# Side work of the heads beside a GEMM: asked for at every GEMM step, or at every fifth step only

## The chip, the cores and the metric

The kernel runs on one core of a Trainium2 chip. The metric is the device time of one execution in microseconds, median over several. The engines are TensorE (PE, with PEld for its weight loads), VectorE (DVE), ScalarE (ACT), GpSimd (POOL) and SyncE (SP, which issues the DMAs).

## The reference

One inference step of a two-layer encoder of width 1024 over 640 rows: 512 of one long sequence and 8 short sequences of 16 rows. Each layer:

```python
h = rmsnorm(x); proj = h @ w_in            # u, va, q|k|v, z, beta, decay, two gates
z_a = gelu(u) * gmlp_spatial(layernorm(gelu(va)))
q, k, v = silu(causal_conv(qkv))           # 8 heads of 128, q and k normalised
o, S = gated_delta_rule(q, k, v, g, beta, s0)
z_b = rmsnorm(o) * silu(z)
x += (sigmoid(ga) * (z_a @ p_a) + sigmoid(gb) * (z_b @ p_b)) @ w_o
x += relu(rmsnorm(x) @ w_up)**2 @ w_down
```

The gated delta rule works per head in four chunks of 128 rows (the kernel's t = 0 to 3) and one tile of the eight short sequences (t = 4). Inside a chunk a unit lower triangular system is solved, then a state S of 128x128 goes from chunk to chunk:

```python
vnew = U - W @ S                 # kS, y, w in the kernel
o    = qg @ S + P @ vnew         # o
S    = S * decay + kg.T @ vnew   # S
```

## The kernel before

GEMMs are made at higher precision: a weight block `raw` (128x1024, one DMA of 512 KB) is split by ScalarE into `whi` (L131) and by VectorE into the rest `wlo` (L132). The activations are split likewise into Ah and Al. `three` then issues for each of 8 k-slices and 2 halves of the columns three matmuls of 128x320: whi by Ah, whi by Al, wlo by Ah. One such triple is a *GEMM step*; a block has 16 steps and a pair of PSUM banks (tag g, two pairs). `Feed` keeps up to two raw tiles loaded ahead and one block split ahead.

The stage `heads` of a layer takes 10 *slots*, h = 0 to 9. A slot has the GEMM blocks of head h (names pg_p, the q, k and v columns, followed by their convolution: cb, then yb at L461, three VectorE passes of 128x664) and some gate blocks (names pg_g, followed by sg at L812). A slot has n = 16 steps for each of its blocks: 64, 112, seven times 80, and 96. Beside the GEMM of slot h run, as Python generators:

- `gating` in slot 0 (decays and betas of all heads),
- `prepare` of head h-1: transposes (ps_kt, kg), the products (ps_gp, AP), a row-wise solve on VectorE (dg, Bs, pr, X), at its end n0c and m16, then the small products Y3 (m16 by q32, copied by ScalarE to y32 at L597) and Z3 (n0c by y32, added to n0c by VectorE at L600). In the profile names these tiles are ps_Y, ps_Z and y. Before the end of prepare the Exp of the next head's decays (E) are issued on ScalarE,
- `chain` of head h-2: the rest of the inverse (Y, M1, Z, Y2, N2), then the recurrence over t: kS, y, w (copied by ScalarE at L662), S with o (the new S is written by VectorE, L734 for t = 0, L732 after). `sample()` runs beside it: kS4, qS4, w4, o4, the scaled copies `we` (ScalarE L699, POOL L700), and S4 in two halves, each added to the state by VectorE (L705),
- `roots` of head h-3: the norm's squares so (L752, L753), their split sh, and means.

Each generator yields a number: how many of its own units the part is that it has just issued. `paced` spreads `length` units (CHAIN 66, PREPARE 70, GATING 48, for roots n; in slot 9 chain and roots in turn, 92) over the n steps of the slot. Before each GEMM step the loop at L913 asks chain, roots and prepare in this order, and each issues what is due. What is left at the slot's end is issued by `run` after the last step. TensorE's instructions stand in the program's order. The other engines' order is set by a scheduler that goes by priority, and `paced` gives side work a lead by `tc.high_priority` (400 for the chain, 200 for prepare and gating, 1 for roots). PSUM banks for the side work: tag c (chain) and tag d (all others), two each.

Of the kernel before, what the change touches and what calls it, by code (L numbers as in the profile page):

```python
# [62 lines left out]
def encoder(ctx, tc, xin, wblk, wba, sct, sdelta, prow, pcol, gates, wst, bsr, convw, consts, delta0,  # L63
# [161 lines left out]
    def paced(work, n, ahead=AHEAD):  # L225


        length, gen = work
        due = 0
        for u in range(n):  # L230
            while due * n <= u * length:
                with tc.high_priority(offset=ahead):
                    due += next(gen, length)
            yield
        run(gen)
# [6 lines left out]
    def run(*gens):  # L242

        for _ in gens[0]:
            for g in gens[1:]:
                next(g, None)
# [562 lines left out]
    def heads(l, ond, msd, gd, close, norm):  # L809
# [70 lines left out]
        with phase(f"heads{l}", 1) as pl:  # L880
# [15 lines left out]
            for h, slot in enumerate(heads_blocks()):  # L896

                n = 16 * len(slot)
                work = []
                if h == H + 1:  # L900
                    work.append(paced((CHAIN + ROOTS, in_turn(
                        chain(l, h - 2, pl, out["gate"], out), lambda: roots(l, h - 2, pl, ond, msd, out))), n, 2 * AHEAD))
                elif h >= 2:
                    work.append(paced((CHAIN, chain(l, h - 2, pl, out["gate"], out)), n, 2 * AHEAD))
                if h >= 3:
                    work.append(paced((n, roots(l, h - 3, pl, ond, msd, out)), n, 1))
                if 1 <= h <= H:
                    work.append(paced((PREPARE, prepare(l, h - 1, pl, act, out["gate"], out)), n))
                if h == 0:
                    work.append(paced((GATING, gating(l, pl, pl, out)), n))  # L910
                for b in slot:
                    stream = gemm(l, b, *how[b])
                    for _ in range(16):  # L913
                        for w in work:
                            next(w)
                        next(stream)
                    run(stream)
                for w in work:
                    run(w)
# [295 lines left out]
```

## Time and profile before

| | us |
|---|---|
| median of three runs | 2545.5 (2544.97 to 2547.24) |
| the profiled execution | 2544.76 |
| its span, first to last instruction | 2543.0 |
| head stage of layer 0, from 54.5 to 569.4 | 514.9 |
| head stage of layer 1, from 1309.0 to 1821.6 | 512.6 |
| TensorE busy over the span | 2471.5 |

All rows of the prediction are from this one execution. A row of the timeline has the start in us, the duration, engine, line, operation, out<-in, the tile's shape and a count; in brackets stands the idle time before it on its engine and what released it. A pair of matmuls of the side work is one row (x2), a group of 16 small ones is one row too (x32, since each counts twice). Matmuls overlap, so the distance of two starts, not the duration, is what one costs. The table of waits has the instruction that waits, what it waits for, the time in all, how often, and the longest.

### The profile page before, as it was taken

What the parts mean: (1) busy time and instruction counts of PE and PEld (TensorE: products, weight loads), DVE (VectorE), ACT (ScalarE), POOL (GpSimd) and SP (SyncE); (2) the same over time, 40 slices, a digit from 0 to 9 for tenths busy, and PEclk for the clock granted to TensorE, in tenths of its full rate; (3) what the DMA queues carried; (4) which work ended last, traced back from release to release, by engine and by line L of the source; (5) the groups of instructions that cost most, each with busy time, mean ns of one, the idle gap of its engine ahead of it and who ended that gap; (6) DMA issues with size and microseconds to landing.
All of it is one profiled execution on the core that took longest, in us unless ns stands there. A gap on an engine that the chain in (4) does not pass through costs nothing. (4 is left out here: it accounts for less than half of the span.)

```text
span 2543.0 us, 45063 instructions
## 1 busy us (share of the span) xinstructions
PE 2471.5 (97%) x18456; PEld 2392.6 (94%) x18456; DVE 1306.3 (51%) x2677; ACT 1011.2 (40%) x1952; POOL 652.6 (26%) x673
## 2 busy tenths in 40 slices
PE   7999999999999999999999999999989999999997
PEld 7899999997899999999999999999979999999997
DVE  7656677535556433333356677674274553333333
ACT  4656666533223212121346666664332222122122
POOL 3223443213422201010213343331253221011012
PEclk9999999999999999999999999999999999999998
DMA  4223433336432222222233333333554322222221
GB/s 161 90 95 101 127 94 95 115 121 229 149 116 75 67 76 76 75 76 75 81 102 108 101 99 95 95 117 117 159 201 142 96 68 76 75 76 76 77 72 66
DMA packets 124238, 261.29 MB, mean 103 GB/s; under 512 B 17232, under 2 KB 56048, under 8 KB 124032
## 3 DMA queue, kind: packets, MB, share of 16 engines
q1 hardware_dynamic: 124032, 258.41, 31.9%
q8 instruction: 145, 2.38, 0.4%
q14 instruction: 61, 0.50, 0.1%
HBM read 218.22 MB, written 40.15 MB: 102 GB/s over the span
## 5 line engine op out<-in xcount | busy, mean ns | idle before, releaser
L131 ACT ACTIVATE whi<-raw 128x1024 fp32r<-128x1024 f32 x304 | 322.1, 1060 | 1012.0 <-issue 367.7
L132 DVE TENSOR_TENSOR wlo<-raw,whi 128x1024 fp32r<-128x1024 f32 x304 | 405.1, 1332 | 161.0 <-ACT whi L131 146.6
L80 PE MATMUL pg_dn<-gl,whi 128*128 128x320 f32 x1024 | 316.6, 309 | 2.1 <-DVE gl L1085 2.1
L80 PE MATMUL pg_up<-Ah,whi 128*128 128x320 f32 x1024 | 317.1, 310 | 0.0
L80 PE MATMUL pg_dn<-gh,whi 128*128 128x320 f32 x1024 | 316.7, 309 | 0.0
L80 PE MATMUL pg_up<-Ah,wlo 128*128 128x320 f32 x1024 | 316.4, 309 | 0.0
L80 PE MATMUL pg_dn<-gh,wlo 128*128 128x320 f32 x1024 | 316.4, 309 | 0.0
L80 PE MATMUL pg_up<-Al,whi 128*128 128x320 f32 x1024 | 316.4, 309 | 0.0
L80 PE MATMUL pg_g<-Ah,whi 128*128 128x320 f32 x896 | 290.8, 325 | 0.0
L80 PE MATMUL pg_g<-Ah,wlo 128*128 128x320 f32 x896 | 278.3, 311 | 7.5 <-DVE wlo L132 7.5
L80 PE MATMUL pg_g<-Al,whi 128*128 128x320 f32 x896 | 277.7, 310 | 0.0
L1084 POOL TENSOR_TENSOR r<-r 128x640 f32<-128x640 f32 x64 | 101.8, 1590 | 684.8 <-ACT gh L1083 684.8
L80 PE MATMUL pg_p<-Ah,whi 128*128 128x320 f32 x768 | 252.1, 328 | 0.0
L80 PE MATMUL pg_p<-Ah,wlo 128*128 128x320 f32 x768 | 237.3, 309 | 0.0
L80 PE MATMUL pg_p<-Al,whi 128*128 128x320 f32 x768 | 236.8, 308 | 0.0
L80 PEld LDWEIGHTS pg_dn<-gl,whi 128*128 128x128 f32 x1024 | 192.2, 188 | 2.6 <-DVE gl L1085 2.6
L80 PEld LDWEIGHTS pg_up<-Al,whi 128*128 128x128 f32 x1024 | 192.2, 188 | 0.0
L80 PEld LDWEIGHTS pg_up<-Ah,whi 128*128 128x128 f32 x1024 | 192.2, 188 | 0.0
L80 PEld LDWEIGHTS pg_dn<-gh,whi 128*128 128x128 f32 x1024 | 192.2, 188 | 0.0
L80 PEld LDWEIGHTS pg_dn<-gh,wlo 128*128 128x128 f32 x1024 | 192.2, 188 | 0.0
L80 PEld LDWEIGHTS pg_up<-Ah,wlo 128*128 128x128 f32 x1024 | 192.2, 188 | 0.0
L80 PEld LDWEIGHTS pg_g<-Ah,wlo 128*128 128x128 f32 x896 | 169.5, 189 | 8.1 <-DVE wlo L132 8.1
(703 smaller groups left out, 5473.5 us busy)
## 6 DMA issues: line engine op xcount, KB each, us to landing
raw<-in_wblk SPq DMA_DIRECT2D x304, 512.0 KB, 3.6
gd<-sg SPq DMA_DIRECT2D x56, 320.0 KB, 2.4
rg<-gd SPq DMA_DIRECT2D x48, 320.0 KB, 2.9
S<-in_sdelta SPq DMA_DIRECT2D x16, 512.0 KB, 6.5
out<-S SPq DMA_DIRECT2D x16, 512.0 KB, 3.5
gr<-rowd SPq DMA_DIRECT2D x16, 320.0 KB, 4.9
er<-rowd SPq DMA_DIRECT2D x16, 320.0 KB, 3.2
ond<-osb SPq DMA_DIRECT2D x16, 320.0 KB, 2.2
```

Of the source, the lines that this page charges most:

```text
L80: nc.tensor.matmul(out, lhsT=lhsT, rhs=rhs, start=start, stop=stop, **kw)
L131: nc.scalar.activation(dst_hi, src, AF.Copy)
L132: nc.vector.tensor_tensor(dst_lo, src, dst_hi.bitcast(F32), op=ALU.subtract)
L1084: nc.gpsimd.tensor_tensor(r[:], r[:], r[:], op=ALU.mult)
```

## The change

`paced` looks whether parts are due at steps 0, 5, 10 and so on only. Parts that fell due at the steps between are issued together at the next such step, for chain, roots, prepare and gating alike, and what fell due after the last such step is issued at the end of the slot.

```diff
@@ paced(work, n, ahead)
         length, gen = work
         due = 0
         for u in range(n):
-            while due * n <= u * length:
+            while u % 5 == 0 and due * n <= u * length:
                 with tc.high_priority(offset=ahead):
                     due += next(gen, length)
             yield
```

In a slot of 80 steps the parts stand at these steps (80 is the slot's end):

| part | before | after |
|---|---|---|
| means (ps_ms), first and second | 8, 18 | 10, 20 |
| first w of the chain | 31 | 35 |
| S and o of t = 0 | 36 | 40 |
| kS of t = 1 | 40 | 40 |
| w, S with o of t = 1 | 45, 50 | 45, 50 |
| w4; o4 | 55; 60 | 55; 60 |
| w of t = 3 with the first half of S4 | 74 | 75 |
| Y3 | 76 | 80 |
| S, o of t = 3, second half of S4 | 79 | 80 |
| Z3 | 80 | 80 |

TensorE at the end of slot 7 of layer 0 (names end in head and chunk; 053 is layer 0, head 5, t = 3, ps_S0541 the second half of S4, kt07 the transposes of the next slot). Before:

```order
L80 MATMUL ps_Y306_5648<-m1606_5613,q32_0_87 32x32 x16
L80 MATMUL pg_g204_5563<-Ah_97,whi_5447 128x320
...
L80 MATMUL pg_g204_5563<-Ah_97,wlo_5448 128x320
L80 MATMUL ps_S053_5676<-w05_5629,kg05_4324 128x128
L80 MATMUL ps_o053_5678<-AP05_4408,w05_5629 128x128
L80 MATMUL ps_o053_5678<-qg05_4530,S052_5572 128x128
L80 MATMUL ps_S0541_5685<-we051_5636,k4p05_5502 128x512 x3
L80 MATMUL pg_g204_5563<-Ah_97,whi_5447 128x320
L80 MATMUL pg_g204_5563<-Al_98,whi_5447 128x320
L80 MATMUL pg_g204_5563<-Ah_97,wlo_5448 128x320
L80 MATMUL ps_Z306_5697<-n0c06_5610,y3206_5665 32x32 x16
L498 MATMUL ps_kt07a_5737<-cst_67,kT07_5149 128x128 x4
```

and after, with the last GEMM matmul of the slot first:

```order
L80 MATMUL pg_g204_5557<-Ah_97,wlo_5445 128x320
L80 MATMUL ps_S053_5663<-w05_5632,kg05_4324 128x128
L80 MATMUL ps_o053_5665<-AP05_4432,w05_5632 128x128
L80 MATMUL ps_o053_5665<-qg05_4539,S052_5566 128x128
L80 MATMUL ps_S0541_5672<-we051_5639,k4p05_5496 128x512 x3
L80 MATMUL ps_Y306_5678<-m1606_5613,q32_0_87 32x32 x16
L80 MATMUL ps_Z306_5697<-n0c06_5610,y3206_5695 32x32 x16
L498 MATMUL ps_kt07a_5737<-cst_67,kT07_5149 128x128 x4
```

All GEMM matmuls of the slot now stand ahead of this group, and nothing stands between Y3 and Z3.

ScalarE at the same place, from the last copy w on. Before:

```order
L662 ACTIVATE w05_5629<-ps_w053_5627 128x128
L131 ACTIVATE sh050_5730<-so05_5727 128x320
L699 ACTIVATE we051_5636<-w4p05_5501,mis_78 128x128 x4
L597 ACTIVATE y3206_5665<-ps_Y306_5648 128x128
L666 ACTIVATE osb05_5282<-ps_o053_5678 128x128
L752 ACTIVATE so05_5727<-osb05_5282 128x320
L131 ACTIVATE k4p06_6166<-kg06_5030 128x128
L131 ACTIVATE whi_5754<-raw_0_70_5451 128x1024
L812 ACTIVATE sg204_5694<-pg_g204_5563 128x640
```

and after:

```order
L662 ACTIVATE w05_5632<-ps_w053_5630 128x128
L752 ACTIVATE so05_5727<-osb05_5317 128x320
L699 ACTIVATE we051_5639<-w4p05_5495,mis_78 128x128 x4
L131 ACTIVATE sh050_5730<-so05_5727 128x320
L131 ACTIVATE whi_5754<-raw_0_70_5448 128x1024
L812 ACTIVATE sg204_5660<-pg_g204_5557 128x640
L131 ACTIVATE k4p06_6160<-kg06_5030 128x128
L666 ACTIVATE osb05_5317<-ps_o053_5665 128x128
L752 ACTIVATE so05_5727<-osb05_5317 128x320
L597 ACTIVATE y3206_5695<-ps_Y306_5678 128x128
```

The copy y32 went behind the next block's split whi, the gate's sg and the last o's copies.

VectorE there, from the last S to the addition of Z3. Before:

```order
L732 SCALAR_TENSOR_TENSOR S053_5681<-S052_5572,dec0_843,ps_S053_5676 128x128
L705 TENSOR_TENSOR S805_5011<-S805_5011,ps_S0541_5685 128x512
L132 TENSOR_TENSOR k4p06_6166<-kg06_5030,k4p06_6166 128x128
L600 TENSOR_TENSOR n0c06_5610<-n0c06_5610,ps_Z306_5697 128x128
```

and after:

```order
L732 SCALAR_TENSOR_TENSOR S053_5668<-S052_5566,dec0_849,ps_S053_5663 128x128
L132 TENSOR_TENSOR wlo_5755<-raw_0_70_5448,whi_5754 128x1024
L132 TENSOR_TENSOR k4p06_6160<-kg06_5030,k4p06_6160 128x128
L705 TENSOR_TENSOR S805_5011<-S805_5011,ps_S0541_5672 128x512
L600 TENSOR_TENSOR n0c06_5610<-n0c06_5610,ps_Z306_5697 128x128
```

The next block's wlo came in ahead of the addition L705, which frees the bank that Z3 takes.

VectorE in slot 1 of layer 1, around the split of the first gate block after the head's own (raw_1_61). Before:

```order
L461 SCALAR_TENSOR_TENSOR yb011_13744<-cb011_13736,cw1_13164,yb011_13744 128x664
L573 TENSOR_TENSOR pr10_13857<-Bs10_13856,X10_13723 128x5x10
L461 SCALAR_TENSOR_TENSOR yb011_13744<-cb011_13736,cw1_13164,yb011_13744 128x664
L576 TENSOR_TENSOR X10_13723<-X10_13723,pr10_13857 128x5x10
L461 SCALAR_TENSOR_TENSOR yb011_13744<-cb011_13736,cw1_13164,yb011_13744 128x664
L573 TENSOR_TENSOR pr10_13857<-Bs10_13856,X10_13723 128x5x9
L132 TENSOR_TENSOR wlo_13752<-raw_1_61_13572,whi_13751 128x1024
```

and after:

```order
L521 SCALAR_TENSOR_TENSOR AP10_13658<-ps_gp102_13681,dsm10_13548,E10_13542 128x256 x2
L461 SCALAR_TENSOR_TENSOR yb111_13632<-cb111_13624,cw1_13164,yb111_13632 128x664
L132 TENSOR_TENSOR k4p10_14632<-kg10_13550,k4p10_14632 128x128
L461 SCALAR_TENSOR_TENSOR yb111_13632<-cb111_13624,cw1_13164,yb111_13632 128x664
L132 TENSOR_TENSOR wlo_13726<-raw_1_61_13572,whi_13725 128x1024
L521 SCALAR_TENSOR_TENSOR AP10_13658<-ps_gp104_13741,dsm10_13548,E10_13542 128x256
L531 SCALAR_TENSOR_TENSOR dg10_13745<-AP10_13658,par_79,dg10_13745 32x80 x4
L567 STREAM_SHUFFLE Bs10_13856<-dg10_13745 128x75
```

This wlo went ahead of the whole row-wise solve (from dg on), which stood ahead of it before.

## The prediction

> **What bounds the kernel now.** I read the page's first two parts, then the windows of the two head stages, then TensorE's list of waits, then the timeline at the places where the new order puts dependent work side by side.
>
> The page, busy time and granted clock over the span:
> ```profile
> PE 2471.5 (97%) x18456; PEld 2392.6 (94%) x18456; DVE 1306.3 (51%) x2677; ACT 1011.2 (40%) x1952; POOL 652.6 (26%) x673
> ...
> PEclk9999999999999999999999999999999999999998
> ```
> The windows of the head stages of layer 0 and layer 1 (us, busy PE, PEld, DVE, ACT, POOL, clock, DMA share, GB/s):
> ```profile
> 54.50:569.40 514.90, 507.31 (x4434) 481.56 (x4433) 312.51 (x962) 309.79 (x735) 160.62 (x229) 1.00 0.34 106
> 1309.00:1821.60 512.60, 507.20 (x4434) 481.69 (x4433) 313.11 (x960) 308.61 (x734) 160.04 (x231) 1.00 0.34 106
> ```
> TensorE is the bound everywhere, in the head stages too (507 of 515 and of 513 us), while VectorE and ScalarE are busy for some 61% there and DMA for a third. TensorE's instructions stand in program order and the change keeps their number. So the time changes only by TensorE waits that come or go. The list of its waits, head stages only (time, times, longest):
> ```profile
> PE pg_g L80 <- DVE wlo L132: 7.5, 2, 4.0
> ...
> PE ps_o L80 <- ACT w L662: 2.5, 10, 0.3
> ...
> PE ps_ms L80 <- ACT kg L505: 1.4, 2, 0.7
> ```
> That is all there is to win; the other waits of the list lie in stages that the change does not touch.
>
> **What goes.** First the two waits for wlo, one in slot 1 of each layer. Timeline, layer 1:
> ```profile
> 1363.55 1.07 ACT L131 ACTIVATE whi<-raw 128x1024 fp32r<-128x1024 f32 x1
> ...
> 1368.42 0.31 PE L80 MATMUL pg_g<-Al,whi 128*128 128x320 f32 x1
> ...
> 1370.98 1.22 DVE L132 TENSOR_TENSOR wlo<-raw,whi 128x1024 fp32r<-128x1024 f32 x1
> ...
> 1372.25 0.42 PE L80 MATMUL pg_g<-Ah,wlo 128*128 128x320 f32 x1 [3.52 <-DVE wlo L132]
> ```
> whi is there at 1364.62, but VectorE comes to wlo at 1370.98 only, because three convolution passes and the row steps of the solve stand ahead of it. In the new VectorE order this wlo stands ahead of the last AP of the head, and the row steps come later. With 1.22 us from 1364.62 it can be done at 1365.9, 2.7 us before TensorE wants it (1368.57). I count both waits as gone. Behind each of them the granted clock is half for one window:
> ```profile
> 119.90:123.30 3.40, 3.30 (x12) 3.30 (x13) 3.40 (x9) 1.23 (x2) 0.25 (x2) 0.50 0.60 181
> 1372.60:1376.00 3.40, 3.40 (x15) 3.40 (x14) 3.40 (x7) 0.79 (x2) 0.00 (x0) 0.50 0.72 236
> ```
> At 0.15 us a GEMM matmul (462.29 to 462.44 in the rows below) 12 and 15 matmuls need 1.8 and 2.25 us, so the half clock costs 1.6 and 1.15, together 2.8. A wait also costs a little more than its idle time: 1368.42 to 1372.25 is 3.83, less the pitch of 0.15 is 3.68 against 3.52 idle, 0.16 each. wlo: 7.5 + 2×0.16 + 2.8 = 10.6 us.
>
> Second, the ten waits for the copy w: ScalarE has the five Exp of the next head's decays ahead of that copy, and in the new order they stand behind it: 2.5 + 10×0.16 = 4.1. Third, the two waits for kg at ps_ms, which moves from step 8 to step 10 (0.88 us later, more than the longest wait of 0.7): 1.4 + 0.3 = 1.7. Sum of the gains: 16.4 us. Ends: nothing (the new order brings other delays to the same copies) and 16.4.
>
> **What comes, (a): S, o and kS in one step.** In a slot of 80 steps the chain's first S and o go from step 36 to step 40, where kS of the next chunk already stood. The 12 GEMM matmuls between S and its user are gone. Rows of before:
> ```profile
> 434.99 0.38 PE L80 MATMUL ps_S<-w,kg 128*128 128x128 f32 x2
> ...
> 435.35 0.39 PE L80 MATMUL pg_p<-Ah,whi 128*128 128x320 f32 x1
> ...
> 435.66 0.29 DVE L734 COPY S<-ps_S 128x128 f32<-128x128 f32 x1
> ...
> 435.98 0.91 DVE L461 SCALAR_TENSOR_TENSOR yb<-cb,cw,yb 128x664 f32<-128x664 f32 x1
> ...
> 437.19 0.38 PE L80 MATMUL ps_kS<-S,kT 128*128 128x128 f32 x2
> ```
> kS could start 0.36 us after S (435.35 less 434.99); VectorE's copy ends 0.96 after S. So TensorE, which has nothing else to take, waits 0.60. The copy there began 0.67 after S behind other VectorE work; the least such delay in the rows is 0.42 (S at 460.92, its update at 461.34, below), a wait of 0.35 to 0.4; with a convolution pass of 0.91 just begun it is 1.5. VectorE is busy 61% of the stage, so I take 0.65. It occurs once for each of the 16 heads. In slot 9 (96 steps) the third S and the kS behind it also meet; there two o pairs lie between, kS could start at 0.58 and the update ends at 0.77: 0.2, twice. Sum 16×0.65 + 0.4 = 10.8 us; ends 6.6 and 24.
>
> **What comes, (b): Y3 and Z3 at the slot's end.** Y3 went out at step 76, four steps ahead of Z3. Now step 76 is not a fifth one, so Y3 waits for the end of the slot, behind the last S, o and S4, and Z3 follows it at once. But Z3 reads y32, ScalarE's copy of Y3, and writes a bank of tag d, which VectorE's addition for S4 (L705) has to free. Rows of before around the end of slot 7:
> ```profile
> 457.23 0.38 PE L80 MATMUL ps_w<-y,n 128*128 128x128 f32 x2
> ...
> 457.68 0.27 ACT L662 ACTIVATE w<-ps_w 128x128 f32<-128x128 f32 x1
> ...
> 458.76 0.47 ACT L131 ACTIVATE sh<-so 128x320 fp32r<-128x320 f32 x1 [0.82 <-POOL so L753]
> ...
> 459.14 1.26 ACT L699 ACTIVATE we<-w4p,mis 128x128 fp32r<-128x128 f32 x4
> ...
> 460.31 0.26 ACT L597 ACTIVATE y<-ps_Y 128x128 f32<-128x128 f32 x1
> ...
> 460.92 0.38 PE L80 MATMUL ps_S<-w,kg 128*128 128x128 f32 x2
> ...
> 461.34 0.35 DVE L732 SCALAR_TENSOR_TENSOR S<-S,dec,ps_S 128x128 f32<-128x128 f32 x1 [1.26 <-PE ps_S L80]
> ...
> 461.50 0.95 PE L80 MATMUL ps_S<-we,k4p 128*128 128x512 f32 x3
> ...
> 461.79 0.28 ACT L666 ACTIVATE osb<-ps_o 128x128 f32<-128x128 f32 x1 [1.22 <-PE ps_o L80]
> ...
> 462.10 0.47 ACT L752 ACTIVATE so<-osb 128x320 f32<-128x320 f32 x1
> ...
> 462.29 0.31 PE L80 MATMUL pg_g<-Ah,whi 128*128 128x320 f32 x1
> ...
> 462.44 0.31 PE L80 MATMUL pg_g<-Al,whi 128*128 128x320 f32 x1
> ...
> 462.49 0.31 ACT L131 ACTIVATE k4p<-kg 128x128 fp32r<-128x128 f32 x1
> 462.49 0.69 DVE L705 TENSOR_TENSOR S<-S,ps_S 128x512 f32<-128x512 f32 x1 [0.80 <-PE ps_S L80]
> ...
> 462.79 1.06 ACT L131 ACTIVATE whi<-raw 128x1024 fp32r<-128x1024 f32 x1
> ...
> 462.83 0.45 PE L80 MATMUL ps_Z<-n0c,y 32*32 32x32 f32 x32
> ...
> 463.10 0.45 DVE L132 TENSOR_TENSOR k4p<-kg,k4p 128x128 fp32r<-128x128 f32 x1
> 463.24 0.66 PE L498 MATMUL ps_kt07a<-cst,kT 128*128 128x128 f32 x4
> ...
> 463.75 0.69 ACT L812 ACTIVATE sg<-pg_g 128x640 f32<-128x640 f32 x1
> ```
> Count from the start of the last S. S4 starts at 0.58 and holds TensorE for 0.79 (461.50 to 462.29), so Y3 starts at 1.37, and Z3 could start at 1.78 (a group of 16 small matmuls takes 0.41, Z3 to kt).
>
> ScalarE's new order from the last copy w on is so, we, sh, whi, sg, k4p, osb, so, y32. w, S4's first half and 15 GEMM matmuls put the last w 3.2 us (0.14 + 0.79 + 15×0.15) ahead of S, and its copy ends 0.72 after it: at −2.45. Adding the durations in that order: so −2.0, we −0.7, sh −0.25, whi 0.8, sg 1.5, k4p 1.8, osb 2.1, so 2.6, y32 2.85.
>
> VectorE's order is now S, wlo, k4p, L705, where before L705 came first. wlo follows whi: 0.8 + 1.22 = 2.0; k4p 2.5; L705 3.2. That one ends last, and Z3 starts at 3.3. Against 1.78 this is 1.5 us; five hand-overs between engines of about 0.04 each (S ends at 461.30, its update starts at 461.34) make it 1.7.
>
> The floor is the copy alone: Y3 at 1.37, 0.67 to the copy as at S, 0.26 for it: Z3 at 2.3, a wait of 0.55. The upper end takes in that sh waits for POOL's so, which now stands behind POOL's we: some 0.7 more, 2.4. For slots 2 to 7 of both layers 12×1.7; slot 8 has no next head whose kt and splits crowd the queue: 2×1.25 (between floor and sum); in slot 1 there is no chain, but y32 stands behind the block's sg, which the block's end releases: 2×1.1. Sum 20.4 + 2.5 + 2.2 = 25.1; ends 16×0.55 = 9 and 16×2.4 = 38.
>
> Other moves cost nothing by these rows: the w, kS4, o4 and S4 groups now meet at steps 45 to 75, each user at least five steps (2.2 us) behind its producer, more than copy and delay (0.96). On SP's queue the side work's loads and stores move past the loads of raw by up to four steps, 1.8 us; two raw tiles are ahead of use, some 14 us (two blocks of 16 steps of 0.44). If that cover is gone, a late whi costs up to the 1.8 us, in a block.
>
> **The sum.** The profiled execution has a span of 2543.0 and took 2544.76. 2544.76 + 10.8 + 25.1 − 16.4 = 2564.3. The median of the runs is 0.74 above the profiled one: 2565 us, slower by 0.8%.
>
> **The rivals.** What counts as no change is within 0.2%, 5.1 us, about what a measurement of this kernel can tell from none.
>
> *The gains stay out.* VectorE and ScalarE keep something else ahead of wlo and w. For it: 61% busy, and five steps of side work arrive at once. Against: the new order has wlo earlier. 2565 + 16.4 = 2581. Chance 0.12.
>
> *The clock drops at the slot's end.* The wait of 1.7 with Y3, Z3 and kt around it is a stretch of 0.41 + 1.5 + 0.41 + 0.66, some 3.1 us, with no GEMM. Each drop costs 1.4 as above, 14×1.4 = 20, 2585. Against it, a plain wait of 2.42 in another stage cost no clock:
> ```profile
> 1851.44 0.50 PE L80 MATMUL pg_va11a<-whi,Ah 128*128 128x512 f32 x1 [2.42 <-ACT vn L945]
> ...
> 1851.40:1858.20 6.80, 6.76 (x30) 5.60 (x31) 5.43 (x9) 3.88 (x6) 1.57 (x1) 1.00 0.92 313
> ```
> and only the waits of 3.5 and 4.0 did. [...] Chance 0.08.
>
> *Only the bare latencies.* ScalarE and VectorE have run their queues down before the slot ends: (b) is its floor of 9. 2545.5 + 10.8 + 9 − 16.4 = 2549, within 0.2%. Against: the eight operations ahead of y32 sum to 5.0 us, and from the end of the last w's copy at −2.45 to the earliest y32 at 2.04 there are 4.5. Chance 0.13.
>
> *Faster.* The 34 new waits are shorter than the gain they displace: TensorE's queue lets S, o and kS overlap as the two matmuls of a pair do. From 0.33 us a wait (11.3 of 34) the kernel is faster by over 5.1; at 0.16 each, the price of a refill alone, it is 2545.5 + 5.4 − 16.4 = 2534.5. Against: a copy by another engine lies between, and the least of its rows is 0.35 to 0.4 net. Chance 0.07.
>
> **How the numbers follow.** The forecast of 2565, its own range 2552 to 2578, has 0.60. Slower: 0.60 + 0.12 + 0.08 = 0.80, same 0.13, faster 0.07. The range 2549 to 2582 leaves out faster, most of the clock's case and a part of same, about 0.18.
>
> **What would show it.** The list of waits after: no ten waits of ps_o for w and no 7.5 us for wlo; instead ps_Z waiting for VectorE's S (L705) or ScalarE's y (L597) some 16 times with 20 to 27 us, and ps_kS for VectorE's S (L734), 16 times, 9 to 12 us. Head stages of about 525 and 522 us, the other stages unchanged. The clock row at 1.00 at the slot ends. I am wrong if ps_Z waits under 0.6 us each, if wlo still makes TensorE wait for microseconds, or if a wait shows up at steps that I priced at nothing, above all for a late raw or whi at a block's start.

## The result and the profile after

The changed kernel takes 2612.4 us (median of five, 2610.7 to 2613.6) against 2545.5: slower by 2.6%, ratio 1.0256 with the interval 1.0245 to 1.0268. The forecast was 2565, so the sign was right and the size was not: 66.9 us instead of 19.5.

The windows of the two head stages of the changed kernel:

```profile
54.20:599.40 545.20, 512.72 (x4434) 486.78 (x4433) 314.39 (x962) 313.60 (x735) 158.53 (x229) 0.98 0.32 100
1340.00:1885.50 545.50, 514.54 (x4434) 488.81 (x4433) 313.42 (x960) 312.52 (x734) 158.60 (x231) 0.98 0.32 99
```

They are 30.3 and 32.9 us longer, 63.2 together, with the same number of TensorE instructions. The clock is 0.98 instead of 1.00, which the forecast did not have. TensorE's waits in these stages:

```profile
PE ps_Z L80 <- ACT y L597: 21.8, 14, 1.7
...
PE ps_kS L80 <- DVE pr L573: 10.8, 12, 0.9
...
PE ps_kS L80 <- DVE S L734: 8.8, 16, 0.8
...
PE ps_kt16a L498 <- DVE S L705: 1.7, 1, 1.7
...
PE ps_kt04a L498 <- DVE S L705: 1.7, 1, 1.7
```

There are twelve such rows of kt, one for each of slots 2 to 7 of both layers. The waits for wlo, for w and at ps_ms are gone from the list, as forecast. Z3 for y32 and kS for the first S are there as forecast. New are the wait of kt for L705, and twelve waits of kS that the profile puts down to the row step pr.

The end of slot 7 of layer 0, the place that was worked out by hand:

```profile
483.59 0.38 PE L80 MATMUL ps_S<-w,kg 128*128 128x128 f32 x2
...
484.09 0.47 ACT L131 ACTIVATE sh<-so 128x320 fp32r<-128x320 f32 x1 [1.14 <-POOL so L753]
...
484.46 1.04 ACT L131 ACTIVATE whi<-raw 128x1024 fp32r<-128x1024 f32 x1
...
484.50 1.55 POOL L541 TENSOR_TENSOR qg<-qT,er 128x640 f32<-128x640 f32 x1 [0.45 <-PE ps_o L80]
...
484.59 1.81 DVE L132 TENSOR_TENSOR sh<-so,sh 128x320 fp32r<-128x320 f32 x1 [1.67 <-ACT sh L131]
...
485.06 0.45 PE L80 MATMUL ps_Y<-m,q 32*32 32x32 f32 x32
...
486.32 0.34 DVE L732 SCALAR_TENSOR_TENSOR S<-S,dec,ps_S 128x128 f32<-128x128 f32 x1
...
486.58 1.21 DVE L132 TENSOR_TENSOR wlo<-raw,whi 128x1024 fp32r<-128x1024 f32 x1
...
486.87 0.26 ACT L597 ACTIVATE y<-ps_Y 128x128 f32<-128x128 f32 x1
...
487.04 1.47 POOL L753 TENSOR_TENSOR so<-so,sq 128x320 f32<-128x320 f32 x1 [0.37 <-ACT so L752]
...
487.18 0.45 PE L80 MATMUL ps_Z<-n0c,y 32*32 32x32 f32 x32 [1.67 <-ACT y L597]
...
487.72 0.94 DVE L132 TENSOR_TENSOR k4p<-kg,k4p 128x128 fp32r<-128x128 f32 x1
...
488.58 0.68 DVE L705 TENSOR_TENSOR S<-S,ps_S 128x512 f32<-128x512 f32 x1
...
489.31 0.90 PE L498 MATMUL ps_kt07a<-cst,kT 128*128 128x128 f32 x3 [1.68 <-DVE S L705]
```

Count from the last S at 483.59. Y3 starts at 1.47 (forecast 1.37) and Z3 at 3.59 (3.3). L705 ends at 5.67, where 3.2 was worked out. Z3 starts 1.40 us before L705 does, right behind the copy y32, so it took the bank that Y3 gave back. L705 does not hold Z3, as the section on the change and the forecast had it; it holds kt, and makes a second wait behind the first.

The twelve kS waits, once (slot 3 of layer 0, S of t = 1 and kS of t = 2, five steps apart):

```profile
177.03 0.38 PE L80 MATMUL ps_S<-w,kg 128*128 128x128 f32 x2
...
179.32 1.23 DVE L132 TENSOR_TENSOR wlo<-raw,whi 128x1024 fp32r<-128x1024 f32 x1
...
180.47 0.34 DVE L732 SCALAR_TENSOR_TENSOR S<-S,dec,ps_S 128x128 f32<-128x128 f32 x1
...
180.96 0.35 PE L80 MATMUL ps_kS<-S,kT 128*128 128x128 f32 x1 [0.90 <-DVE pr L573]
```

kS reads the S of 180.47, which ends at 180.81. That S was ready to be computed from about 177.4, but stands behind row steps and wlo in VectorE's order. The pr that the profile names is only what ended next to it.

The clock: windows of 3.41 us that follow each other, at two slot ends of the changed kernel (slots 7 and 2 of layer 0), and around the plain wait of 2.42 us that the prediction used, in the kernel before:

```profile
485.76:489.17 3.41, 0.45 (x32) 0.34 (x32) 3.41 (x5) 1.96 (x6) 2.31 (x4) 1.00 0.41 159
489.18:492.59 3.41, 3.28 (x14) 3.28 (x15) 1.53 (x7) 2.13 (x12) 0.00 (x0) 0.50 0.75 226
...
195.63:199.04 3.41, 1.74 (x60) 1.22 (x62) 2.76 (x3) 3.01 (x7) 2.53 (x5) 1.00 0.33 119
199.04:202.45 3.41, 1.73 (x43) 1.62 (x34) 3.36 (x9) 1.46 (x5) 1.16 (x1) 1.00 0.68 222
```
```profile
1847.06:1850.47 3.41, 1.97 (x9) 1.31 (x7) 3.41 (x3) 0.72 (x2) 2.39 (x2) 1.00 0.38 114
1850.47:1853.88 3.41, 2.44 (x11) 2.02 (x12) 3.21 (x6) 3.01 (x6) 0.00 (x0) 1.00 0.89 293
```

The half-clock windows of one run lie on one grid of 3.41 us. At the end of slot 7 both waits fall into one window; TensorE is busy for 0.45 us of it, and the next window has half the clock. At the end of slot 2, with the same waits, the grid's border cuts them in two; each window has 1.7 us of work, and the clock stays. The wait of 2.42 us was cut the same way. Eleven of the twelve slot ends got a half-clock window; the kernel before had two such windows in its head stages, both behind wlo.

### The profile page after: what moved, and what is told of

Same layout as the page of the kernel before. It is cut to its first block, busy times and chain, and to the rows that moved or that the text cites. A ratio compares the mean times of both kernels' runs of the same rounds, so it can differ in the third digit from the quotient of the medians.

```text
span 2608.9 us, 45048 instructions
## 1 busy us (share of the span) xinstructions
PE 2489.2 (95%) x18456; PEld 2408.7 (92%) x18456; DVE 1315.8 (50%) x2677; ACT 1019.6 (39%) x1952; POOL 644.8 (25%) x673
## 5 line engine op out<-in xcount | busy, mean ns | idle before, releaser
L80 PE MATMUL pg_p<-Al,whi 128*128 128x320 f32 x768 | 242.2, 315 | 0.0
L80 PEld LDWEIGHTS pg_g<-Ah,whi 128*128 128x128 f32 x896 | 169.5, 189 | 5.4 <-issue 3.5
```

Source lines behind the costliest of these rows:

```text
L80: nc.tensor.matmul(out, lhsT=lhsT, rhs=rhs, start=start, stop=stop, **kw)
```

## The experiments

Theory A: what costs is which dependent parts meet, and whose copy or bank they wait for on ScalarE and VectorE; two waits at the slot's end are separate, and the half clock follows from their idle time. The main rivals: B, that kt is late only because Z3 was; C and D, that the clock drops by the kind of work at the slot's end; E, that five steps' parts at once cost by themselves. Ratios are to the kernel before, on the same chip.

**Y3 at step 75.**
```diff
-   paced((PREPARE, prepare(l, h - 1, ...
+   paced((PREPARE + (h > 1), prepare(l, h - 1, ...
```


> The kernel after, but in slots 2 to 8 prepare counts 71 units instead of 70, so that Y3 goes out at step 75 and not at the slot's end; the last S, o, S4 and Z3 stay at the end. Theory A (two separate late parts: y32 stands late on ScalarE, and the addition L705 stands late on VectorE behind wlo and two k4p; each alone would hold TensorE): the wait of Z3 for y32 goes (12 x 1.7 us), but L705 still ends some 5.5 us after the last S, so the wait of kt for it grows from 1.7 to about 3.5 us, the half clock behind it stays in 12 slots, and the time is within 6 us of the kernel after, about 2612. Rival B (Y3 directly ahead of Z3 is the cause, and kt is late only because Z3 was): both waits (12 x 3.4 = 41) and the half clock (12 x 1.5 = 18) go: about 2553.

2599.0 us, ratio 1.0204 (1.0189 to 1.0220).
```profile
PE ps_kt03a L498 <- DVE S L705: 2.5, 1, 2.5
```
Z3's wait has left the list and kt's went from 1.7 to 2.5 us, twelve times. B is out: with Z3 on time, kt waits longer. A had the direction and not the size: of the 3.4 us of both waits 2.5 were left, and of the eleven half-clock windows nine, so 13 us were won where A said at most 6.

**The chain asked at every step.**
```diff
-   paced((CHAIN, chain(...)), n, 2 * AHEAD)    # and chain + roots in slot 9
+   paced((CHAIN, chain(...)), n, 2 * AHEAD, 1) # new last argument: asked at every step; without it, at every fifth
```


> The kernel after, but the chain (in slot 9 with roots) is asked at every step as before; prepare, roots and gating at every fifth. The last S is at step 79 again, one GEMM step ahead of Y3 and Z3; the addition L705 stands ahead of wlo on VectorE; S and o of t = 0 are at step 36 again, kS at 40. Theory A: kS of t = 1 waits no more for S (minus 16 x 0.65 = 10), kt waits no more for L705 (minus 12 x 1.7 = 20), the half clock goes as the lull gets shorter than 3 us (minus 18), Z3 still waits for y32 by 1.5 to 2 us, and kS of t = 2 still waits 1.05 us in 12 slots since the new S stands behind wlo on VectorE: about 2564. Rival B (kt is late because Z3 is): only the first goes, about 2602. Rival C (the clock drops for lack of GEMM work at the slot's end, whatever the waits): the half clock stays, about 2582.

2569.6 us, 1.0089 (1.0074 to 1.0104).
```profile
PE ps_Z L80 <- ACT y L597: 19.2, 12, 1.6
...
PE ps_kS L80 <- DVE pr L573: 11.2, 12, 1.2
```
As A said to within 6 us: kS for the first S and kt for L705 are gone, Z3 and the kS of t = 2 stay. Of the eleven half-clock windows three are left, although the slot's end keeps its small matmuls and transposes, so C is out too. No run shows the 3 us of the expectation as a border: in the kernel before the clock stayed full at a wait of 2.42 us and was half behind one of 3.52, and in the changed kernel it was half behind two waits of 1.7 us that fell into one window.

**Prepare asked at every step.** The same edit on the line of prepare.

> The kernel after, but prepare is asked at every step as before; chain, roots and gating at every fifth. Y3 is at step 76 again, VectorE has the row-wise solve ahead of the chain's second S as before, and in slot 1 wlo stands late again. Theory A: Z3 waits no more; kt waits for L705, which still stands behind wlo and k4p, by about 3.5 us, with the half clock (no net change at the slot's end); kS of t = 2 waits no more (minus 12.6); the two wlo waits of slot 1 are back (plus 10.6): about 2610. Rival B: slot ends without waits and half clock (minus 59): about 2551.

2596.0 us, 1.0192 (1.0175 to 1.0209).
```profile
PE pg_g L80 <- DVE wlo L132: 9.0, 2, 4.8
...
PE ps_kt05a L498 <- DVE S L705: 2.5, 1, 2.5
```
The twelve waits of kS for the late second S go. (The list still has twelve waits of kS, 10.1 us, put down to a row step X: these stand right behind o and are the waits for the first S, 0.8 us each instead of 0.5.) wlo is late again, and kt waits 2.5 us as with Y3 at step 75. So wlo's gain and the twelve kS waits both belong to prepare's row-wise solve, which comes later when prepare is asked at every fifth step. A was 14 us too high, most of it by the same 2.5 instead of 3.5.

**Slot 1 alone.** The kernel before, with every fifth step only for prepare of slot 1.

> The kernel before with every fifth step for prepare in slot 1 alone; all other slots as before. Theory A: there wlo goes ahead of the row-wise solve on VectorE, and the two waits of 3.5 and 4.0 us with their half clock go (10.6 us), against 1 us twice for Y3 and Z3 side by side at the end of slot 1: about 2537. Rival: wlo is late for another reason (its raw tile or whi), and the time stays at 2545 to 2548.

2533.0 us, 0.9946 (0.9931 to 0.9961). Windows of its head stages:
```profile
54.18:562.96 508.78, 505.57 (x4435) 480.08 (x4433) 313.60 (x962) 311.42 (x736) 160.69 (x229) 1.00 0.34 108
1300.80:1807.85 507.05, 505.35 (x4434) 480.10 (x4433) 312.19 (x960) 310.25 (x735) 160.58 (x231) 1.00 0.34 107
```
6.1 and 5.6 us shorter, and neither has a half-clock window. The gain of the change is real, and it lies in one slot of ten.

**Extra matmuls in the waits, first try.** Ten matmuls of 128x320 by Ah alone, into unused columns of the Y3 and Z3 banks.

> The kernel after with ten extra GEMM-sized matmuls (128x320) at the ends of slots 2 to 7: six between Y3 and Z3 and four between Z3 and kt, into parts of the Y3 and Z3 banks that nothing reads. They add 120 matmuls, 17.6 us of TensorE work, all inside the two waits, whose ends (y32 and L705) they do not move. Theory A (the half clock there is set by how much TensorE idles in a clock window of 3.41 us): the 10 half windows of the head stages (14 us net in the sum) go and nothing else changes: about 2598, in spite of the added work. Rival D (the half clock comes from the kind of work at the slot's end, transposes and small matmuls, or costs nothing because it lies beside waits): the time stays at 2612 or goes up to 2630 by the added work.

2630.9 us, 1.0328 (1.0314 to 1.0342).
```profile
PE ps_Z L80 <- ACT y L603: 36.8, 14, 2.9
```
Inconclusive: the edit moved y32 behind sq in ScalarE's order, the wait of Z3 grew to 2.9 us, and the windows were still half idle; 18 got the half clock.

**Extra matmuls, y32 in its place.** Six and eight of them, and a third buffer for sq, which keeps y32 ahead of sq.
```diff
+   def filler(b, n):
+       if 1 <= h <= 6:                         # slots 2 to 7
+           for _ in range(n):
+               mm(b[:, P:P + 320], Ah[:, 0, 0:P], Ah[:, 0, 0:HT], True, True)
...
    by, b = joined(Q32, m16, f"Y3{nm}")
+   filler(b, 6)
...
    bz, b = joined(y32, n0c, f"Z3{nm}")
+   filler(b, 8)
-   sq = pl.tile([P, 5, P], F32, tag="sq", bufs=2, ...)
+   sq = pl.tile([P, 5, P], F32, tag="sq", bufs=3, ...)
```


> The kernel after with a third buffer for sq and extra GEMM-sized matmuls at the ends of slots 2 to 7: six between Y3 and Z3, eight between Z3 and kt (168 in all, 25 us of TensorE work), into parts of banks that nothing reads. y32 keeps its place on ScalarE, so the two waits end where they did. Theory A (idle time of TensorE in a clock window sets the half clock): under 1.2 us of each window is idle, the half windows of the head stages go, and in spite of 25 us of added work the time falls to about 2598. Rival D (the half clock comes with the kind of work, or lies beside waits and costs nothing): 2612 to 2637.

2593.0 us, 1.0186 (1.0170 to 1.0201).
```profile
54.78:592.94 538.16, 520.19 (x4519) 491.94 (x4517) 314.22 (x962) 312.64 (x735) 159.16 (x229) 1.00 0.33 102
1332.16:1868.92 536.76, 520.25 (x4519) 491.99 (x4517) 314.26 (x960) 311.43 (x734) 159.24 (x231) 1.00 0.33 101
```
168 more matmuls, and 19 us less than the changed kernel. No head window has the half clock. The edit has two parts, but the third buffer did not shorten the two waits: at the end of slot 7, Z3 starts 3.58 us and kt 5.75 us after the last S, as in the changed kernel (3.59 and 5.72). So the half clock came from idle time. The head stages are 15.8 us shorter, which is what eleven half-clock windows cost, about 1.4 us each. D is out.

**Asked at the last step too.**
```diff
-   while u % 5 == 0 and due * n <= u * length:
+   while (u % 5 == 0 or u == n - 1) and due * n <= u * length:
```


> The kernel after, but paced asks at the slot's last step too (every fifth step and step n-1), so the last S, o, S4 and Y3 go out at step 79, one GEMM step ahead of Z3 and kt. Theory A: VectorE has L705 ahead of wlo again, so kt waits no more for it (minus 21) and the half clock goes (minus 14); Z3 waits for y32 by about 0.9 us instead of 1.7 (minus 9); the kS waits stay: about 2569. Rival E (parts that come five steps at once are what costs, wherever the last ones stand): no more than the wait of one GEMM step is won in each slot, 16 x 0.44 = 7 us: about 2605.

2588.4 us, 1.0164 (1.0149 to 1.0180). Between the two. kt's wait is gone, but Z3 waits 2.3 us for y32 and eight half-clock windows stay. ScalarE and POOL at that slot's end:
```profile
482.09 0.55 POOL L554 COPY qb<-qg 128x64 f32<-128x64 f32 x2
...
482.60 0.86 POOL L753 TENSOR_TENSOR so<-so,sq 128x320 f32<-128x320 f32 x1
...
483.49 0.74 ACT L602 ACTIVATE sq<-qT 128x640 f32<-128x640 f32 x1 [1.68 <-POOL so L753]
...
484.13 0.26 ACT L597 ACTIVATE y<-ps_Y 128x128 f32<-128x128 f32 x1
```
y32 stands behind sq, and sq waits 1.68 us for POOL's so, which reads the buffer that the new sq is to take.

**The last step, and a third buffer for sq.**

> The kernel that is asked at the last step too, with a third buffer for sq (the norm's square at L601), so that ScalarE has y32 straight behind the last k4p and no longer behind sq, which waited for POOL's so to give its buffer back. Theory A (Z3 waits for ScalarE's queue, not for the distance of one step): the wait of Z3 falls from 2.3 us to 0.2 or so in 12 slots (minus 26) and the half clock goes (minus 10): about 2553. What is left above the kernel before is then the kS waits (22) less the gains (14). Rival E (five steps' parts at once cost by themselves): less than 10 us is won, 2580 or more.

2565.6 us, 1.0077 (1.0061 to 1.0094).
```profile
PE ps_Z L80 <- DVE S L705: 15.2, 12, 1.3
```
No head window has the half clock any more, and y32 is no longer waited for; but the next one in line, L705, now holds Z3 by 1.3 us, which makes the 13 us between 2553 and 2566. E is out: the parts still come five steps at once, and 47 us of the loss are gone.

**Other steps of the same grain.**
```diff
-   while u % 5 == 0 and due * n <= u * length:
+   while u % 5 == 4 and due * n <= u * length:
```


> The kernel after, but asked at steps 4, 9, 14 and so on instead of 0, 5, 10: the same grain, other collisions. S of t = 0 is at 39 and kS of t = 1 at 44, so these part; the last S, o, S4 and Y3 are at 79, one GEMM step ahead of Z3; kS of t = 3 now meets its own w at step 74. Theory A (what costs is which dependent parts meet in one step): kS waits for the first S no more, slot ends wait for y32 only (12 x 0.9), the new pair kS, w waits for y by about 0.8 us in 16 heads (13), kS of t = 2 as in the kernel after (12): about 2568. Rival E (the grain of five costs): about the kernel after, 2605 to 2612.

2630.7 us, 1.0329 (1.0315 to 1.0343): slower than either forecast.
```profile
PE ps_w L80 <- DVE y L714: 29.4, 18, 2.1
...
PE ps_Z L80 <- ACT y L597: 26.3, 12, 2.2
...
PE pg_g L80 <- ACT whi L131: 4.9, 2, 2.5
```
The collision that A named (kS with its own w) is there in place of kS with S, at twice the price that was set, with Z3 behind y32 and sq as above, and 17 half-clock windows. So the grain alone does not fix the price, but A had the collisions and not their sizes, which were far too low.

**Slot 1 and roots.** As slot 1 alone, and roots at every fifth step.

> The kernel before with every fifth step for prepare in slot 1 and for roots in slots 3 to 8; all else as before. Theory A: as the kernel with slot 1 alone (2533), less the two waits of the means for kg, whose step goes from 8 to 10 (1.7 us): about 2531. Rival: roots' parts in larger pieces delay the copies of the slot's end, and it is 3 us slower than that.

2530.2 us, 0.9937 (0.9925 to 0.9950). The two waits of ps_ms are gone from the list. This version beats both kernels, by 16.5 and 82 us. Its 2.8 us below the kernel with slot 1 alone lie within the two intervals; that the roots gain is read from the list.

**A third buffer for qg.** In the changed kernel, and in the one asked at the last step too.
```diff
-   qg = pl.tile([P, 5, P], F32, tag="qg", bufs=2, ...)
+   qg = pl.tile([P, 5, P], F32, tag="qg", bufs=3, ...)
```


> The kernel after with a third buffer for qg, so that POOL's product qg (L541, 1.55 us) no longer waits for the last o of the slot to give a buffer back and runs some steps earlier. VectorE's and ScalarE's orders stay. Theory F (VectorE's sh and k4p took 1.81 and 0.94 us at the slot's end, instead of 0.48 and 0.28, because POOL worked beside them; that made L705 late): sh is back at 0.5 us, L705 ends some 1.3 us earlier, the wait of kt for it falls from 1.7 to 0.4 us (minus 15), and part of the half windows goes (minus 10): about 2587. Rival G (L705 is late by its place behind wlo and whi alone): kt still waits 1.7 us, 2608 to 2615.

> The kernel that is asked at the last step too, with a third buffer for qg. There Z3 waits 2.3 us for y32, which stands behind sq, which waits for POOL's second so, which stands behind POOL's qg and the qb copies. Theory A with POOL in the chain: with qg gone from there so runs 1 us earlier, y32 too, Z3 waits 1.3 us instead of 2.3 (minus 12), and most of the half windows go (minus 10): about 2566. Rival G (POOL is not in that chain): within 4 us of 2588.

2625.4 us, 1.0308 (1.0291 to 1.0326), and 2619.5 us, 1.0287 (1.0272 to 1.0302): both slower, where both theories had faster or the same. VectorE at the slot's end, and TensorE's waits, of the first:
```profile
495.72 0.49 DVE L132 TENSOR_TENSOR sh<-so,sh 128x320 fp32r<-128x320 f32 x1 [1.67 <-ACT sh L131]
...
498.01 0.68 DVE L705 TENSOR_TENSOR S<-S,ps_S 128x512 f32<-128x512 f32 x1
```
```profile
PE ps_Z L80 <- ACT y L597: 31.1, 14, 2.8
...
PE ps_S L80 <- POOL we L700: 19.3, 10, 2.3
```
The part of F about VectorE is right: with qg elsewhere, sh takes 0.49 us instead of 1.81, at the end of slot 7 of layer 0 L705 ends 3.96 us after the last S (at 494.73) instead of 5.67, and kt waits no more, with Z3 at the same 3.58. G is out: L705's place behind whi and wlo is the same. But qg now stands ahead of POOL's we, and the second half of S4 waits for we, ten times, 2.3 us at most; POOL had no room at that place either. The half-clock windows went up from 11 to 21 in the first of the two kernels and from 8 to 20 in the second.

## Why the prediction was wrong

The sum, term by term. Measured is the time that TensorE's transitions of that kind took above their usual distance in both head stages, after less before.

| term | forecast | measured |
|---|---|---|
| wlo of slot 1 with its half clock | −10.6 | −11.1 |
| w ahead of o | −4.1 | −4.1 |
| kg ahead of ps_ms | −1.7 | −1.7 |
| (a) S, o, kS in one step | +10.8 | +8.9 |
| (b) Y3 and Z3, Z3's wait | +25.1 | +23.6 |
| kt behind L705 | 0 | +21.0 |
| kS of t = 2 behind a late S | 0 | +12.7 |
| half clock at slot ends | 0 (rival: 20) | +17.6 |
| sum | +19.5 | +66.9 |

In the two profiled executions the head stages grew by 63.2, so the table is 3.7 too high there; that its sum equals the difference of the medians is chance. Some of the 3.7 lies in the half-clock term: the extra matmuls took the half clock away, and the head stages won 15.8 by it and not 17.6. The rest of the program, whose code is the same, grew by 2.7, and this was not traced to a cause.

1. The gains: right in place and in size; the kernel with slot 1 alone shows the largest by itself.

2. Term (a) is right in mechanism and near in size. Term (b) is right in size by luck. The 1.7 us were worked out as a wait of Z3 for L705, with y32 ready at 2.85 and not the last to come. What held Z3 was y32, which ended at 3.54: ScalarE's sh waited 1.14 us for POOL's so and ended at 0.97 instead of −0.25, and whi and all behind it were late by it. The forecast had this delay, at 0.7, in its upper end only.

3. The step that failed first is the sentence "L705 3.2. That one ends last, and Z3 starts at 3.3". It made one wait of two. L705 ended at 5.67, 2.47 later than worked out, and held kt and not Z3. Its working had three errors. VectorE's sh, which stands ahead of the last S in its order, was left out of the sum. Its duration was not constant: 1.81 us with POOL's qg beside it, 0.49 us when qg was moved away; k4p took 0.94 instead of 0.45, beside POOL's so. And whi ended at 1.91 instead of 0.8, by the late sh of ScalarE. The run with a third buffer for qg divides the 2.47: without POOL beside VectorE L705 ended at 3.96, so 1.7 us came from that, and the other 0.8 go with the late whi. The upper end "2.4" in the prediction names POOL, but only as something that sh waits for on ScalarE.

4. "Each user at least five steps (2.2 us) behind its producer, more than copy and delay (0.96)", so at no cost: this failed for kS of t = 2. The delay of 0.42 to 0.67 was read at two places where little stood ahead; in the new order VectorE has ten row steps and a wlo there, 3.4 us from S to its update. Asking prepare at every step took these waits away, so the later row steps are the cause. The new VectorE order is shown at two places of the section on the change, and neither is this one.

5. The clock rival, at 0.08, came true beside the second wait, at 16 to 18 us of the 20 that it gave; its one stretch of 3.1 us was in fact two waits of 1.7. What spoke against it, the plain wait of 2.42 us at full clock, was no evidence: the grid's border cut that wait in two, into windows with 1.97 and 2.44 us of work. The kernel before shows the grid too: its two half-clock windows, at 119.90 and 1372.60, are 1252.7 us apart, 367 windows of 3.413 us; with it the row that I set against the rival could have been read rightly. Nor did it take one long wait: two waits of 1.7 us in one window, with 0.45 us of work left in it, were enough.

6. A reading that cost nothing: TensorE's list of waits before has one more in the head stage of layer 0, pg_ba for cb, 1.5 us, where the prediction says that the other waits lie elsewhere. It is unchanged after.

The forecast's own sign that it would be wrong, "if a wait shows up at steps that I priced at nothing", is what the list of waits showed.

## What to carry to other kernels

When parts are moved so that a producer and its user meet, work out the queue of every engine between them from the new order, not only the copy's own time, and go on to the next user: taking one wait away showed or lengthened the next one in several kernels here. Price a wait together with the clock that it may cost, by how much work is left in its window and not by the length of one wait: here, of the windows of 3.41 us counted in the next section, each with less than 1.49 us of work was followed by the half clock, and none with more than 1.77. And look for the part of a change that gains: with the change in one slot of ten alone the kernel was 14 us faster than before (11.7 in the head stages), and the kernel with the change there and for roots has the lowest time of all.

## What the runs showed of the hardware

In these runs the half clock had a narrow border. Over the head stages of all fourteen profiles, taking the grid windows with more than 0.9 us of TensorE idle time that were themselves at full clock: 93 were followed by a half-clock window, and TensorE was busy for 1.77 us or less in each of them; 114 were not, and it was busy for 1.49 us or more. Between 1.49 and 1.77 us both occur, so in these runs the border is at about half of the 3.41 us. In the kernel before and the changed one alone, 13 were followed by a half-clock window (busy for 1.30 us or less) and 12 were not (1.73 us or more). Work that was put into the idle time paid for itself here: 168 added matmuls made the kernel 19 us faster.

VectorE's sh, a subtraction of two SBUF tensors, took 0.49 us where POOL's qg had been moved away, and 1.81 us in the changed kernel, where this product of two SBUF tensors ran for 1.55 us over nearly all of it; sh ended 0.35 us after qg did. By what mechanism is not shown. POOL's so took 1.47 us instead of 0.87 where VectorE's wlo had started first (the profile's spans on POOL are rough). VectorE's L705, which reads PSUM and SBUF, took 0.69 us beside qg in the kernel before (qg from 461.83 to 463.39) and 0.68 without it. The kernel before showed the effect at the same place, in a row that the prediction does not have:
```profile
458.69 1.04 POOL L700 TENSOR_TENSOR we<-w4p,mis 128x512 fp32r<-128x512 f32 x1
...
459.27 0.81 DVE L132 TENSOR_TENSOR sh<-so,sh 128x320 fp32r<-128x320 f32 x1 [0.17 <-ACT sh L131]
```
Its cost is easily overlooked, because the profile shows VectorE as busy for the whole 1.81 us.
